# Queries and keys projected transposed, with even and odd columns apart, and rotated there

## The chip, the cores and the metric

The kernel runs on one core of one Trainium2 chip. Its time is the device time of one execution in microseconds (us), given as the median of several runs. The engines are TensorE (PE: matmuls and transposes), VectorE (DVE), ScalarE (ACT), GpSimd (POOL) and SyncE (SP), which issues most of the DMA transfers. The profile comes from one execution of its own.

## The reference

A transformer of four layers works on 1024 latent tokens and 256 context tokens of width 1024, in float32. Layers 0 and 3 are "banded": 16 query heads of 64 in four groups, each group with one key and value head, attention over a window of 128 tokens to either side and over the context, with a sink. Layer 1 is "latent": queries from a rank of 256, with 64 rotary dimensions in each of 8 heads. Layer 2 is an mLSTM. Queries and keys of latent tokens are rotated in pairs of neighbouring columns; context tokens are not rotated. The last layer needs no outputs for the context.

```python
def apply_rope(x, cos, sin):
    x1, x2 = x[..., 0::2], x[..., 1::2]
    cos, sin = cos[:, None, :], sin[:, None, :]
    return jnp.stack([x1 * cos - x2 * sin, x1 * sin + x2 * cos], axis=-1).reshape(x.shape)
...
    def block(n):
...
        logits = jnp.einsum('bqkgd,bjkd->bkgqj', q_b, k_b).astype(jnp.float32) * scale
        p = sink_softmax(jnp.where(mask, logits, NEG_INF), sink_l)
        return jnp.einsum('bkgqj,bjkd->bqkgd', p.astype(v_b.dtype), v_b)
...
    y_l = (o_l * jax.nn.silu(z_l)) @ w_out
```

## The kernel before

A float32 product is made of three matmuls on parts of type float32r: high by high, high by low and low by high (`split` makes the parts, one engine the high and another the low one). The normed input lies transposed in the on-chip memory for the whole layer, `hT` = (`hh`, `hl`), channels on partitions and 1280 tokens in a row. Weights come in as pieces of 512 KB, in one stream whose order `plan` fixes; `step` splits a piece into `wh` and `wl`, `need` takes pieces up to a given chunk, and a `pacer` does so bit by bit between other work. The columns of the modulation (`mod_piece`, tiles `raw` and `cs`) come in the same stream. Code is written in one order, and a scheduler then sets each engine's own order from it.

A banded layer (`layer_a`) has these stages. Keys and values: for each of ten token tiles of 128, 24 matmuls of 512 columns give keys and values token by token. `rope` rotates the keys (a VectorE product with the cosine, two with the sine and an add on GpSimd), `kv_back` splits them, and a tile later `kv_tr` transposes high and low parts (8 transposes, an ACT copy) and stores them to DRAM (`kd`). In layer 0 the norm of the input tiles (`first_norm`) feeds these tiles one by one, and the pacer takes up gate columns of the modulation and the first z weights between them. Then come eight z blocks (`z_block`), and then group 0's queries.

The attention runs over units (group, token tile): ten tiles in each of four groups in layer 0, eight in layer 3. Unit s does scores and weights (`stage_s`) while unit s - 1 transposes its weights and multiplies them by the values (`stage_pv`). Between the parts `fill` puts steps of the next group's query projection (`proj_q`): 24 matmuls of 256 columns for a token tile, three to a step. The projected tile is rotated by `rope` and stored row by row (`qd`). For each unit `load_q` brings its queries back two units ahead, and `stage_q` splits them (`q2`), transposes them for four heads, and copies them to `qT`, [128 = high and low parts of 64 dimensions, 4 heads x 128 tokens]. In the last group there is nothing to project; the output weights are split in its place.

In the latent layer (`layer_b`) `uq_front` and `uq_back` project, rotate, split and transpose the rotary queries of all heads for one token tile at a time, between the z blocks: eight transposes a tile.

## Time and profile before

| | us |
|---|---|
| median of 3 runs | 3097.39 |
| lowest and highest | 3097.36, 3098.17 |
| span of the profiled execution | 3100.0 |
| TensorE busy in it | 2904.0 |
| VectorE, ScalarE, GpSimd busy | 1751.2, 1315.9, 1271.3 |

The span runs from the first to the last instruction of the profiled execution; no other time is known of that execution, and its span is 2.6 us above the median of the runs. A busy engine need not be a full one: matmuls overlap, so the distance from one start to the next tells more than their durations. A stretch is a part of the span in which one stage runs, and an idle engine has a releaser, the work whose end it waited for.

### The profile page before, as it was taken

The numbers are of one execution on the slowest core, as the hardware profiler recorded it, in microseconds if no ns is written. First come the engines' busy times: TensorE is split into PE (matmuls) and PEld (weight loads), VectorE is DVE, ScalarE is ACT, GpSimd is POOL, SyncE is SP. The second block draws the span as 40 slices with busy tenths as digits, with TensorE's granted clock in tenths as the row PEclk, the third lists the DMA queues.
The fourth block names the chain that finished last, engine by engine and source line by source line (L and its number), as shares of the span: only waits on it lengthen the run. The fifth ranks groups of instructions, "written<-read, shape, count | busy, mean of one in ns | idle before, by whom it ended". The sixth has DMA issues, their size and how long they took to land. (4 is left out here: it accounts for less than half of the span.)

```text
span 3100.0 us, 51341 instructions
## 1 busy us (share of the span) xinstructions
PE 2904.0 (94%) x18340; PEld 2542.3 (82%) x18340; DVE 1751.2 (56%) x4001; ACT 1315.9 (42%) x2812; POOL 1271.3 (41%) x1584
## 2 busy tenths in 40 slices
PE   7999999999999999999898999998888999999998
PEld 4788888778888788888787899998776778988877
DVE  3413877875522466666456644244497742588862
ACT  2311776763322355555433323132364431367662
POOL 2413666655643010100454331246574532466652
PEclk9999999999999999999999999999898999999999
DMA  7563222434246211111443344688576545232313
GB/s 230 177 195 109 73 77 88 143 116 133 90 150 187 78 43 33 33 40 32 129 143 118 118 148 134 212 292 292 196 244 214 180 129 176 70 93 88 103 60 119
DMA packets 404386, 409.52 MB, mean 132 GB/s; under 512 B 29506, under 2 KB 351322, under 8 KB 403106
## 3 DMA queue, kind: packets, MB, share of 16 engines
q1 hardware_dynamic: 398816, 399.25, 40.3%
q10 hardware_dynamic: 4882, 6.33, 0.6%
q8 instruction: 145, 2.38, 0.3%
q0 software_dynamic: 432, 0.66, 0.1%
q14 instruction: 111, 0.91, 0.1%
HBM read 275.46 MB, written 131.34 MB: 131 GB/s over the span
## 5 line engine op out<-in xcount | busy, mean ns | idle before, releaser
L89 DVE TENSOR_TENSOR pl<-n,ph 128x512 fp32r<-128x512 f32 x488 | 330.4, 685 | 94.6 <-ACT ph L80 79.7
L80 ACT ACTIVATE ph<-n 128x512 fp32r<-128x512 f32 x488 | 285.1, 596 | 156.9 <-PE n L75 92.0
L72 PE MATMUL n<-ph,v 128*128 128x256 f32 (+1 forms) x992 | 292.3, 337 | 15.1 <-ACT ph L80 9.0
L75 PE MATMUL n<-ident,p 128*128 128x128 f32 x1952 | 289.5, 277 | 8.5 <-DVE o L846 4.8
L72 PE MATMUL n<-wh,hh 128*128 128x256 f32 x960 | 278.4, 290 | 16.3 <-DVE sg L1659 11.7
L812 POOL TENSOR_SCALAR p<-p,rl 128x640 f32<-128x640 f32 (+2 forms) x288 | 215.8, 762 | 167.1 <-DVE rl L810 114.1
L72 PE MATMUL n<-wl,hh 128*128 128x256 f32 x960 | 275.4, 287 | 0.0
L72 PE MATMUL n<-wh,hl 128*128 128x256 f32 x960 | 275.1, 287 | 0.0
L805 ACT ACTIVATE p<-p,nm 128x641 f32<-128x641 f32 (+2 forms) x288 | 220.7, 767 | 121.7 <-DVE nm L803 111.0
L75 PEld LDWEIGHTS n<-ident,p 128*128 128x128 f32 x1952 | 234.6, 142 | 43.7 <-issue 10.8
L72 PE MATMUL n<-pl,v 128*128 128x512 f32 (+1 forms) x656 | 241.6, 368 | 9.7 <-DVE pl L89 8.7
L801 DVE CUSTOM_DVE_ANT_0 p<-w,mask 128x640 f32<-128x640 f32 (+2 forms) x288 | 209.5, 744 | 60.3 <-PE w L72 51.6
L72 PE MATMUL n<-hh,wh 128*128 128x512 f32 (+1 forms) x656 | 242.1, 369 | 0.0
L89 POOL TENSOR_TENSOR wl<-raw,wh 128x1024 fp32r<-128x1024 f32 x54 | 135.9, 2521 | 253.6 <-DVE wh L82 180.5
L72 PE MATMUL n<-hl,wh 128*128 128x512 f32 (+1 forms) x656 | 238.4, 363 | 0.0
L72 PE MATMUL n<-hh,wl 128*128 128x512 f32 (+1 forms) x656 | 238.2, 363 | 0.0
L72 PE MATMUL w<-ks,qT 128*128 128x256 f32 (+1 forms) x1088 | 204.0, 316 | 17.9 <-DVE mx L801 13.5
L1232 POOL TENSOR_TENSOR o<-o,z 128x256 f32<-128x256 f32 x40 | 30.4, 760 | 447.5 <-ACT o L1231 204.2
L72 PEld LDWEIGHTS n<-wh,hh 128*128 128x128 f32 x960 | 187.8, 196 | 20.3 <-DVE sg L1659 12.7
L72 PEld LDWEIGHTS n<-ph,v 128*128 128x128 f32 x992 | 175.6, 190 | 29.6 <-ACT ph L80 17.6
L72 PEld LDWEIGHTS w<-ks,qT 128*128 128x128 f32 x1088 | 172.6, 192 | 29.5 <-DVE mx L801 18.4
L72 PEld LDWEIGHTS n<-wl,hh 128*128 128x128 f32 x960 | 187.8, 196 | 0.1
(333 smaller groups left out, 7598.3 us busy)
## 6 DMA issues: line engine op xcount, KB each, us to landing
raw<-in_l_w_ada_dram SPq DMA_DIRECT2D x96, 512.0 KB
raw<-in_l_w_in_dram SPq DMA_DIRECT2D x72, 512.0 KB
raw<-in_l_w_out_dram SPq DMA_DIRECT2D x32, 512.0 KB
vd<-v SPq DMA_DIRECT2D x60, 256.0 KB
xd<-xt SPq DMA_DIRECT2D x30, 512.0 KB
od<-o SPq DMA_DIRECT2D x112, 128.0 KB
go<-od SPq DMA_DIRECT2D x28, 512.0 KB
xt<-xd SPq DMA_DIRECT2D x28, 512.0 KB
```

What stands on the lines that cost most here:

```text
L72: self.nc.tensor.matmul(out, lhsT, rhs, start=start, stop=stop)
L75: self.nc.tensor.transpose(out, in_, self.ident)
L80: nc.scalar.activation(out=out, in_=in_, func=AF.Copy)
L89: e.tensor_tensor(out=lo, in0=src, in1=as32(hi), op=ALU.subtract)
L801: nc.vector.tensor_tensor_reduce(out=p[:, 0:n], in0=ps[:, s0:768], in1=mask[:, mo:mo + n], scale=1.0, scalar=-3.0e38, op0=ALU.add, op1=ALU ...
L805: nc.scalar.activation(out=p[:, 0:n + 1], in_=p[:, 0:n + 1], func=AF.Exp, scale=0.125, bias=nm[:, j:j + 1], accum_out=lsum[:, j:j + 1])
L812: nc.gpsimd.tensor_scalar(out=pr[y][:, 0:n], in0=pr[y][:, 0:n], scalar1=rl[:, y:y + 1], scalar2=0.5, op0=ALU.mult, op1=ALU.mult)
L1232: nc.gpsimd.tensor_tensor(out=o, in0=o, in1=z, op=ALU.mult)
```

## The change

The weights of keys, queries and rotary queries are put into another column order when they are split: first the even dimensions of all heads, then the odd ones (`Chunk.eo`, `take`). With these as the fixed operand and `hT` as the moving one, a matmul gives [128 = 4 heads x 32 even dimensions, up to 512 tokens]. The pieces of tokens are `PIECES` = ((0, 512), (512, 512), (1024, 256)). `eo_even` copies the even half out of PSUM; `eo_odd` multiplies the odd half by sine and cosine on VectorE (tables laid out transposed, `cosT` and `sinT`) and the even half on GpSimd, combines them, splits both results into high and low parts (`eo_h`, `eo_l`, one buffer each) and stores each part to DRAM. `load_q` and `load_group` put them together as [parts and halves, heads, tokens], so that `rope` on queries, `kv_back`, `kv_tr`, `stage_q`, `uq_front` and `uq_back` fall away. The values are still projected token by token, with 256 columns; the keys follow in pieces, in `keys`. In layer 0 the z weights get their place, and the pacer starts, only after the last tile. A step of `fill` is now one matmul.

```diff
-        qd = [self.pd.tile([T, 256], F32, name=f"qd{i}_{g}") for g in range(4)]
-        kd = self.pd.tile([4, 128, 2, T], F32, name=f"kd{i}")
+        qd = [self.pd.tile([4, 128, T], F32, name=f"qd{i}_{g}") for g in range(4)]
+        kd = self.pd.tile([4, 128, T], F32, name=f"kd{i}")
...
+    def take(self, ch, rv, k0, s, hi, lo):
+        k = slice(k0, k0 + s)
+        eo = ch.eo
+        if eo:
+            def paired(a):
+                a = a[:, :, 0:eo] if eo < ch.n else a
+                return a if eo == 256 else a.rearrange("p k (a c) -> p (k a) c", c=256)
+            o = [paired(w[:, k]).rearrange("p k (b j) -> p k b j", b=2) for w in (ch.wh, ch.wl)]
+            self.split(o[0], o[1], paired(rv).rearrange("p k (j b) -> p k b j", b=2), hi, lo)
+        if eo < ch.n:
+            self.split(ch.wh[:, k, eo:ch.n], ch.wl[:, k, eo:ch.n], rv[:, :, eo:ch.n], hi, lo)
...
+    def eo_even(self, pool, ps, t0, n):
+        e = pool.tile([128, 512], F32, name="eo_e", bufs=1)
+        self.nc.scalar.activation(out=e[:, 0:n], in_=ps[:, 0:n], func=AF.Copy)
+        return e
+
+    def eo_odd(self, pool, e, ps, t0, n, put):
+        nc = self.nc
+        e, ps = e[:, 0:n], ps[:, 0:n]
+        lat = t0 < NLAT
+        if lat:
+            c, sn = self.cosT[:, t0:t0 + n], self.sinT[:, t0:t0 + n]
+            x = [pool.tile([128, 512], F32, name=f"eo_t{x}", bufs=1)[:, 0:n] for x in range(3)]
+            nc.vector.tensor_tensor(out=x[0], in0=ps, in1=sn, op=ALU.mult)
+            nc.vector.tensor_tensor(out=x[1], in0=ps, in1=c, op=ALU.mult)
+            nc.gpsimd.tensor_tensor(out=x[2], in0=e, in1=sn, op=ALU.mult)
+            nc.gpsimd.tensor_tensor(out=e, in0=e, in1=c, op=ALU.mult)
+            nc.gpsimd.tensor_tensor(out=e, in0=e, in1=x[0], op=ALU.subtract)
+        for b in range(2):
+            hi, lo = [pool.tile([128, 512], F32R, name=f"eo_{x}", bufs=1)[:, 0:n] for x in "hl"]
+            if b and lat:
+                nc.vector.tensor_tensor(out=x[2], in0=x[2], in1=x[1], op=ALU.add)
+            self.split(hi, lo, e if b == 0 else x[2] if lat else ps, "act", "pool" if b == 0 or lat else "dve")
+            for p, y in ((b, hi), (b + 2, lo)):
+                nc.sync.dma_start(out=put(p)[:, t0:t0 + n], in_=as32(y))
...
-        pend = None
+        def keys(t0, n):
+            w = P["kv"]
+            e = None
+            for b in range(2):
+                ps = self.psn()
+                self.proj_T(ps[:, 0:n], hT, w.wh, w.wl, 128 * b, 128, t0, n)
+                if b == 0:
+                    e = self.eo_even(qp, ps, t0, n)
+                else:
+                    self.eo_odd(qp, e, ps, t0, n, lambda p: kd[p])
+
+        stretches = {1: [PIECES[2]], 5: [PIECES[0]], 9: [PIECES[1]]}
+        if i:
+            stretches = {1: [PIECES[2]], 9: [PIECES[0], PIECES[1]]}
...
+            if n == (1 if i else NT - 1):
...
                 pz = self.pool("pz", hs)
                 for x in range(8):
                     P["z", x].place(pz, 2)
-                go = self.pacer(NT - 2, P["z", 0])
-            elif n:
+                go = self.pacer(NT - 2 if i else 1, P["z", 0])
+            elif n > 1 and i:
                 go()
+            for x in stretches.get(n, ()):
+                keys(*x)
+        go()
...
-        fs, fp = ((3, 2, 2, 0), (0, 1, 0, 0, 0)) if need_ctx else ((2, 2, 2, 0), (0, 2, 0, 0, 0))
+            for t0, m in ((PIECES[2],) if need_ctx else ()) + PIECES[:2]:
+                e = None
+                ts = slice(t0, t0 + m)
+                for b in range(2):
+                    ps = self.psn()
+                    c = slice(128 * b, 128 * b + 128)
+                    for k in range(8):
+                        for x, (a_, b_) in enumerate(((w.wh, hh), (w.wh, hl), (w.wl, hh))):
+                            self.mm(ps[:, 0:m], a_[:, k, c], b_[:, k, ts], k == 0 and x == 0, k == 7 and x == 2)
+                            if k < 7 or x < 2:
+                                yield
+                    if b == 0:
+                        e = self.eo_even(qp, ps, t0, m)
+                    else:
+                        self.eo_odd(qp, e, ps, t0, m, lambda p: qd[g][p])
+                    yield
+
+        fs, fp = ((5, 4, 3, 0), (0, 2, 0, 0, 0)) if need_ctx else ((4, 3, 3, 0), (0, 2, 0, 0, 0))
...
         def load_q(u):
...
-            q = p2.tile([128, 4, 64], F32, name="qin", bufs=2)
-            nc.sync.dma_start(out=q, in_=qd[g][t * 128:(t + 1) * 128, :].rearrange("p (h d) -> p h d", d=64))
+            q = p2.tile([128, 4, 128], F32R, name="qT", bufs=2)
+            for p in range(4):
+                nc.sync.dma_start(out=as32(q[32 * p:32 * p + 32]),
+                                  in_=qd[g][p, :, t * 128:(t + 1) * 128].rearrange("(h i) t -> i h t", i=32))
```

In the attention of layer 0, TensorE's order has a run of query projections (`wqh` and `wql` the weights' parts) between the scores of a unit (`w<-ks,qT`) and the products with the values (`ph`, `pl` by `v`). Before, the run is 24 long at this place and of 256 columns, and the transposes of the next unit's queries come soon after:

```order
L72 MATMUL n<-ph,v_2187 128x512
L72 MATMUL n<-wqh,hh 128x256
L72 MATMUL n<-wql,hh 128x256
...
L72 MATMUL n<-wqh,hl 128x256
L72 MATMUL w<-ks,qT 128x384 x2
L72 MATMUL w<-ks,qT 128x256 x2
L72 MATMUL n<-pl,v_2187 128x512
L72 MATMUL n<-ph,v_2187 128x512
L75 MATMUL n<-ident,q_2935 128x128 x4
```

After, at the same place, the run is 19 long and of 512 columns:

```order
L73 MATMUL w<-ks,qT 128x384 x2
L73 MATMUL w<-ks,qT 128x256 x2
L73 MATMUL n<-pl,v_2142 128x512
L73 MATMUL n<-ph,v_2142 128x512
L73 MATMUL n<-hh,wqh 128x512
L73 MATMUL n<-hl,wqh 128x512
L73 MATMUL n<-hh,wql 128x512
...
L73 MATMUL n<-hh,wqh 128x512
L73 MATMUL n<-pl,v_2142 128x512
L73 MATMUL n<-ph,v_2142 128x512
L76 MATMUL n<-ident,p 128x128 x4
```

The transposes of queries are gone; the runs are wider, and there are fewer of them.

ScalarE's order in the same attention has the copy and the split of the queries among the exponentials (`p,lsum<-p,nm`) and the copies of the transposed weights (`ph<-n`). Before:

```order
L805 ACTIVATE p,lsum<-p,nm 128x641 x2
L765 ACTIVATE qT<-n 128x512
L80 ACTIVATE q_3084<-qin 128x4x64
L805 ACTIVATE p,lsum<-p,nm 128x641
L841 ACTIVATE up<-n 64x512
L80 ACTIVATE ph<-n 128x512 x2
```

After, `eo_h<-eo_e` is the high part of a piece's even half and `eo_h<-eo_t` that of its odd half:

```order
L81 ACTIVATE ph<-n 128x512 x3
L81 ACTIVATE eo_h<-eo_e 128x512
L81 ACTIVATE ph<-n 128x512
L81 ACTIVATE eo_h<-eo_t_4435 128x512
L81 ACTIVATE ph<-n 128x512
L852 ACTIVATE p,lsum<-p,nm 128x641 x2
```

The two high parts go into one buffer, with one weight copy between them.

At the end of layer 0's keys, TensorE's order after the change has the last keys (`wkvh`, `wkvl`), then modulation columns (`raw,cs`), then the first z block (`hh,wh`); before, the modulation columns stood between the tiles:

```order
L73 MATMUL n<-hh,wkvl 128x512
L73 MATMUL n<-raw,cs 32x256 x8
L73 MATMUL n<-sel,part 128x2 x2
L73 MATMUL n<-raw,cs 32x256 x4
...
L73 MATMUL n<-raw,cs 32x256 x4
L73 MATMUL n<-sel,part 128x2 x2
L76 MATMUL n<-ident,gc 16x128
L73 MATMUL n<-hh,wh 128x512
```

The modulation's last columns have moved behind the keys.

## Rows read from the trace of the kernel before

**Rows 1.** The profile's page: the span, the busy time of each engine with its share and instructions, and the chain that ended last by engine and line.
```profile
span 3100.0 us, 51341 instructions
PE 2904.0 (94%) x18340; PEld 2542.3 (82%) x18340; DVE 1751.2 (56%) x4001; ACT 1315.9 (42%) x2812; POOL 1271.3 (41%) x1584
...
PE n L72 18%; PE w L72 6%; PE n L75 3%; DVE acc L1328 1%; DMA e<-rmd 1%; DMA raw<-in_l_w_in_dram 1%; DVE cl L89 1%; POOL hl L89 1%; DMA kt<-ktd 1%; DVE big L374 1%; DMA gdd<-e 1%; DMA sgd<-sg 0%; DVE p L801 0%; DVE go L1782 0%; DMA dT<-gdd 0%
```

**Rows 2.** Busy time by stretch. Columns: start and end, length, busy us and instructions of PE, PEld (weight loads), DVE, ACT and POOL, then the granted TensorE clock, the DMA engines' mean busy share and GB/s. The stretches in turn: keys and values of layer 0, its group 0's queries, its attention for groups 0 to 2, most of the latent layer's z blocks, keys and values of layer 3, its attention for groups 0 to 2, and its last group.
```profile
49.10:137.30 88.20, 82.20 (x458) 66.36 (x458) 45.65 (x135) 32.05 (x60) 46.40 (x42) 0.94 0.58 171
...
259.20:288.60 29.40, 29.36 (x246) 29.12 (x244) 6.54 (x24) 1.57 (x5) 5.90 (x8) 1.00 0.18 60
288.60:610.00 321.40, 306.76 (x2148) 275.97 (x2149) 257.68 (x743) 220.95 (x499) 201.70 (x356) 0.97 0.28 88
...
845.00:1000.00 155.00, 153.29 (x940) 127.34 (x940) 43.80 (x121) 38.73 (x91) 64.27 (x73) 1.00 0.54 166
2525.40:2576.10 50.70, 50.70 (x250) 41.91 (x250) 10.67 (x35) 12.61 (x30) 10.67 (x14) 1.00 0.46 129
...
2682.00:2901.70 219.70, 213.84 (x1554) 198.71 (x1555) 180.91 (x512) 156.27 (x336) 140.88 (x238) 1.00 0.27 84
2901.70:2991.00 89.30, 75.91 (x452) 64.22 (x451) 74.42 (x180) 59.79 (x130) 64.23 (x92) 0.92 0.30 95
```

**Rows 3.** TensorE's own sequence in layer 3's attention: start, duration, engine, line, operation, output and inputs, shapes, count. The first row is the four transposes of a unit's queries.
```profile
2707.80 0.60 PE L75 MATMUL n<-ident,q 128*128 128x128 f32 x4
2708.15 0.48 PE L72 MATMUL n<-ph,v 128*128 128x512 f32 x1
```

**Rows 4.** The same view: the end of layer 0's z blocks with the start of its query projection, 256 columns each, and 512 columns in layer 3's z blocks.
```profile
259.04 0.28 PE L72 MATMUL n<-hh,wl 128*128 128x256 f32 x1
259.16 0.28 PE L72 MATMUL n<-wqh,hh 128*128 128x256 f32 x1
...
2599.80 0.39 PE L72 MATMUL n<-hh,wh 128*128 128x512 f32 x1
...
2600.93 0.39 PE L72 MATMUL n<-hh,wl 128*128 128x512 f32 x1
```

**Rows 5.** TensorE's waits at the start of the attention, in layer 0 (260 to 300 us) and in layer 3 (2580 to 2685): the line that waited, what ended the wait, total us, number, longest.
```profile
PE w L72 <- ACT qT L765: 3.4, 2, 2.7
PE n L75 <- POOL q L89: 1.3, 1, 1.3
...
PE n L75 <- POOL q L89: 0.8, 1, 0.8
PE w L72 <- ACT qT L765: 0.7, 1, 0.7
```

**Rows 6.** TensorE's sequence over one tile of layer 3's keys and values, from the transposes of one tile's keys (`k`) to those of the next.
```profile
2537.40 1.04 PE L75 MATMUL n<-ident,k 128*128 128x128 f32 x8
...
2538.51 0.40 PE L72 MATMUL n<-wkvl,hh 128*128 128x512 f32 x1
...
2543.64 0.39 PE L72 MATMUL n<-wkvh,hl 128*128 128x512 f32 x1
2543.88 1.03 PE L75 MATMUL n<-ident,k 128*128 128x128 f32 x8
```

**Rows 7.** A group of like instructions over the whole span: count, busy us, mean ns of one, idle time of the engine just before. These are the transposes of queries, 288 in the two banded layers and 80 in the latent one.
```profile
L75 PE MATMUL n<-ident,q 128*128 128x128 f32 x368 | 61.1, 278 | 3.6 <-POOL q L89 3.6
```

**Rows 8.** One tile's norm in layer 0, on three engines: the modulation, the high part and the low part.
```profile
85.27 2.65 DVE L374 TENSOR_SCALAR big<-n,mod 128x128 f32<-128x128 f32 x8
...
87.95 1.06 ACT L80 ACTIVATE hh<-big 128x1024 fp32r<-128x1024 f32 x1 [1.76 <-DVE big L374]
...
89.09 2.39 POOL L89 TENSOR_TENSOR hl<-big,hh 128x1024 fp32r<-128x1024 f32 x1 [1.59 <-ACT hh L80]
```

**Rows 9.** Pieces of the chain that ended last: start, us from issue to landing, and the transfer. A weight piece of 512 KB, a store of 256 KB, and a store of queries of 128 KB.
```profile
1732.41 4.39 DMA raw<-in_l_w_in_dram
...
1876.35 2.13 DMA vd<-v
...
2918.40 6.08 DMA qd<-q
```

**Rows 10.** Groups of like instructions, by shape: over the whole span, and the last two rows over 300 to 600 us.
```profile
L245 POOL TENSOR_TENSOR q<-rope,rope 128x512 f32<-128x512 f32 x8 | 10.3, 1289 | 41.4 <-DVE rope L243 41.4
...
L238 DVE TENSOR_TENSOR rope<-n,cos 128x512 f32<-128x512 f32 x8 | 5.5, 692 | 15.5 <-PE n L72 15.5
...
L238 DVE TENSOR_TENSOR rope<-n,cos 128x256 f32<-128x256 f32 x80 | 33.8, 423 | 86.8 <-PE n L72 81.1 <-PE n L75 5.2
...
L243 DVE TENSOR_TENSOR rope<-n,sin 128x128 f32<-128x128 f32 x160 | 38.8, 282 | 0.0
...
L80 ACT ACTIVATE ph<-n 128x512 fp32r<-128x512 f32 x127 | 73.4, 595 | 20.1 <-DVE pl L89 6.8 <-DVE rl L810 5.5 <-PE n L75 4.0
...
L89 POOL TENSOR_TENSOR q<-qin,q 128x256 fp32r<-128x256 f32 x31 | 23.8, 767 | 11.1 <-ACT q L80 5.0 <-PE n L75 3.0 <-PE n L72 2.3
```

**Rows 11.** SyncE's issues of a unit's output, in layer 0's last group: one a unit.
```profile
653.18 0.46 SPq L848 DMA_DIRECT2D od<-o  x1
...
662.98 0.52 SPq L848 DMA_DIRECT2D od<-o  x1
```

More of the change, by code (lines that the diff above doesn't have):

```diff
@@ L286, in setup, with tables @@
         self.xd = self.pd.tile([T, D], F32, name="xd")
+    def tables(self, pool):
+        self.cosT = pool.tile([128, NLAT], F32, name="cosT")
+        self.sinT = pool.tile([128, NLAT], F32, name="sinT")
+        self.nc.scalar.dma_start(out=self.cosT, in_=self.ins["k_cosT"])
+        self.nc.scalar.dma_start(out=self.sinT, in_=self.ins["k_sinT"])
     def load_cols(self, i, queue):
@@ L742, in load_group @@
             ks = p2.tile([128, 2, T], F32R, name="ks", bufs=2)
-            nc.sync.dma_start(out=as32(ks), in_=kd[g])
+            for x in range(2):
+                for p in range(4):
+                    nc.sync.dma_start(out=as32(ks[32 * p:32 * p + 32, x]), in_=kd[(p + 2 * x) % 4, 32 * g:32 * g + 32, :])
             v2 = p2.tile([128, NT, 128], F32R, name="v2", bufs=2)
@@ L754, in load_q @@
                               .rearrange("(a p) t -> p a t", p=128))
-            st[u] = {"q": q, "z": z}
-        def stage_q(u):
-            q = st[u]["q"]
-            q2 = p3.tile([128, 4, 128], F32R, name="q2", bufs=1)
-            self.split(q2[:, :, 0:64], q2[:, :, 64:128], q, "act", "pool")
-            pt = self.psn()
-            for h in range(4):
-                self.tr(pt[:, h * 128:(h + 1) * 128], as32(q2[:, h, :]))
-            qT = p3.tile([128, 4, 128], F32R, name="qT", bufs=2)
-            nc.scalar.activation(out=qT, in_=pt[:, :].rearrange("p (h t) -> p h t", h=4), func=AF.Copy)
-            st[u]["qT"] = qT
+            st[u] = {"qT": q, "z": z}
         def cols(t):
@@ L889, in layer_a @@
                     load_group(units[s][0] + 1)
-                if s + 2 < nu and s + 2 not in st and (s + 2) % nq >= 2:
-                    load_q(s + 2)
                 stage_s(s, fill)
@@ L1079, in proj_q @@
             qp = p2.tile([128, 512], F32R, name="qp", bufs=2)
-            nc.sync.dma_start(out=as32(qp[:, 0:n]), in_=qpd[h, :, s])
+            for x in range(4):
+                nc.sync.dma_start(out=as32(qp[32 * x:32 * x + 32, 0:n]), in_=qpd[x, 32 * h:32 * h + 32, s])
             for t in range(t0 // 128, (t0 + n) // 128):
@@ L1098, in layer_b @@
         done = set()
-        uq = deque(ORDER)
-        upend = pu = None
+        uq = deque((hb, t0, n) for (t0, n) in PIECES for hb in range(2))
+        pu = None
         slot = 0
```

133 lines of the change are left out of this document (51 added, 82 removed).

## The prediction

> **What bounds the kernel now.** I read the page first: TensorE is busy for 94% of the span, and the chain that ended last runs through its matmuls more than through anything else [rows 1]. A share over the whole span says little, so the table of stretches came next [rows 2]. It splits into two kinds. The keys and values of the last layer, the z blocks of the latent layer and the first projection of a group of queries are dense: TensorE is busy for 50.70 of 50.70 us, 153.29 of 155.00 and 29.36 of 29.40. The attention of groups 0 to 2 is nearly dense, with 306.76 of 321.40 us in layer 0 and 213.84 of 219.70 in layer 3, at a granted clock of 0.97 and 1.00; VectorE comes second there (257.68 and 180.91). What is taken off TensorE in these places should come off the time. The other kind is the last group of queries, which has no projection between its units: 75.91 of 89.30 us on TensorE, 74.42 on VectorE. Nobody is full there and I count nothing for it. The keys and values of layer 0 are a third case (82.20 of 88.20), since a chain over three engines feeds them. Last I read the waits at the two places where the scores of group 0 begin, and single rows for the durations.
>
> **What the change removes.** *Transposes of queries.* Each unit loses four on TensorE, the split of its queries and the copy back. In the stream the four take 0.35 us, from 2707.80 to the next matmul at 2708.15 [rows 3]. Layer 0 has 30 units in groups 0 to 2 and layer 3 has 24: 54 x 0.35 = 18.9 us. The 18 units of the two last groups are set at nothing, because TensorE waits there anyway; at full worth they would be 6.3 more.
>
> *Projection of queries.* The moving operand grows from 256 columns to 512, except for the 256 context tokens. A matmul of 256 columns follows the one before after 0.12 us, one of 512 after (2600.93 - 2599.80) / 5 = 0.226 [rows 4]. A group of layer 0 goes from 240 x 0.12 = 28.8 us to 96 x 0.226 + 48 x 0.12 = 27.5, one of layer 3 from 192 x 0.12 = 23.0 to 96 x 0.226 = 21.7. Eight groups at 1.3 give 10.4 us. The keys of layer 3 show 0.233 for 512 columns [rows 6], at which the term is 5; the queries have the weights on the side where the z blocks have them, so I take 0.226. A rule speaks against the change here: the Trainium skill, page "TensorE: Matmul & The Clock Gate", section "Back-to-back issue gap", puts an isolated gap at N / 2.4 + 2.5 ns, by which I estimate 109 ns for 256 columns and 216 for 512, and half the instructions would save 0.25 us a group, 2 us in all. The trace has 120 and 226 and doesn't agree at 256.
>
> *The start of the attention.* TensorE now waits 3.4 + 1.3 us in layer 0 and 0.8 + 0.7 in layer 3 for the first queries to be split, transposed and copied [rows 5]. After the change they come ready from memory. In layer 0 the context piece is projected first, 2 x 10.9 us before group 0's projection ends, so the 4.7 us go. In layer 3 the first piece has 10.9 us, and its rotation, split, store (2.13) and load add up to about as much; I leave that wait where it is.
>
> *Keys.* In layer 3 a tile takes 6.48 us (2537.40 to 2543.88), and 24 matmuls at (2543.64 - 2538.51) / 22 = 0.233 are 5.60 of it; eight transposes are the other 0.88 [rows 6]. The columns of the matmuls stay the same: 24 of 512 a tile become 24 of 256 for the values and 48 for each piece of keys. The first two tiles wait for weights, which leaves 8 x 0.88 = 7.0 us.
>
> *Rotary queries of the latent layer.* 80 of the 368 transposes [rows 7] lie in a dense stretch, at 0.35 / 4: 7.1 us.
>
> *Keys of layer 0.* TensorE loses ten times 0.88, 8.8 us. But a tile's norm runs VectorE 2.65, ScalarE 1.06 and GpSimd 2.39 us in a row [rows 8], and the modulation's eight gate pieces, which lay between the tiles, now stand behind them with the first z weights. A 512 KB piece takes some 4.4 us to land [rows 9], and three are there in advance; casting the z piece and its low part adds 3. I estimate a tail of 12 us behind the last key matmul. That matmul would end near 49.1 + 82.2 - 8.8 = 122 and z begin near 134, against 137.3: 3.3 us gained. The bounds are 8.8 gained (the tail hidden) and 8.7 lost (a tail twice as long).
>
> Sum of gains: 18.9 + 10.4 + 4.7 + 7.0 + 7.1 + 3.3 = 51.4 us.
>
> **What it adds.** *Work off TensorE.* A piece of 512 tokens asks GpSimd for three products and two low parts at 1.29 us each [rows 10], 6.4 us, and VectorE for three at 0.69, which is 0.52 a tile where the old rotation had 0.42 and two of 0.28 (0.98). ScalarE loses a copy and a split a unit and gets three copies of 0.6 a piece, 0.45 a tile. GpSimd drops a split and an add of 0.77 each a tile for 1.6, so it stays where it is, at 0.63 of the stretch. All this lies under TensorE and costs nothing while TensorE is the bound. If that cover went, GpSimd's 6.4 us would stand in front of one store, needed half a group later.
>
> *Single buffers.* This is the cost I do charge. The rotated halves leave through one buffer for the high and one for the low part. The second half's high part, on ScalarE, must wait until the first half's store has landed. In the new order one weight copy of 0.6 us lies between the two on ScalarE, and on GpSimd nothing. Behind the waiting instruction stand the copies of the weights, and TensorE waits for those. A store of 256 KB, the size of these, landed in 2.13 us, a store of 128 KB in 6.08 [rows 9]. From the nearest row: 2.13 + 0.35 to issue - 1.0 of work between = 1.5 us. About half of the 15 pieces projected inside the attention have so little between: 7 x 1.5 = 11 us. Bounds: nothing, if ScalarE has that much slack (it is busy for 220.95 of 321.40 us), and 7 x 5.5 = 38.
>
> *Evenness.* Now a unit has one run of about 18 projection matmuls, 2.2 us; then a run is 19 of 512 columns, 4.3 us, every 1.8 units. During a run the softmax gets no scores. A unit without projection takes 9.8 us in the last group (653.18 to 662.98) [rows 11]; less 0.5 for the rotation, 9.3. Say u is the part of a run that nothing covers. Now 9.8 + 2.2 u = 541.1 / 54 = 10.0, so u is 0.1; then 9.3 + 4.3 u / 1.8 = 9.55 at the same u. TensorE's own sum gives 10.0 - 0.35 - 10.4 / 54 = 9.46. I take no extra cost.
>
> *Queues.* SP issues five transfers a unit for two, and four stores a piece for four row stores; at 0.4 to 0.5 us each that is 2.5 us of a unit of 10. Queries are loaded two units ahead, so a load that stands behind a waiting store has some 9 us to spare.
>
> 51.4 - 11 = 40.4 us. The profiled execution has a span of 3100.0 us, 2.6 above the median of 3097.4; the differences are taken from its rows and set against the median: 3097.4 - 40.4 = 3057.0 us. A difference under 0.2%, 6.2 us, can't be told from no change.
>
> **Rivals.**
> *Stores block ScalarE and GpSimd for their longest landing.* For it: the stores and the loads of queries share one queue, and 6.08 us occurs. Against it: DMA engines are 28% busy in that stretch. Price 38 instead of 11: 3084 us. It decides nothing about the sign. The Trainium skill, page "DMA: Bandwidth & Descriptors", section "Anatomy of one DMA — SWDGE (gpsimd) path", gives some 2 us of fixed cost to each transfer, mostly the receipt of the write. The 2.13 us row agrees.
> *Long runs starve the softmax (the slower side).* If u rises to 0.5, a unit takes 9.3 + 1.2 = 10.5, and 54 units lose 27 us while the other stretches gain 17.4: 3107 us. It decides from u = 0.43 on, which is 0.3 us a unit lost. For it: VectorE would be at 0.85 of the time between runs, and only two score buffers hold work. Against it: nine weight buffers, and u is 0.1 now.
> *A long tail behind layer 0's keys.* Modulation and the first z weights in a row, nothing beside them: 8.7 lost for 3.3 gained, 3069 us. For it: one modulation chunk can't be multiplied before it has landed, and TensorE has no other work there.
> *Wide matmuls bring nothing.* If the 0.12 us comes from what stands around these matmuls and not from their width, those of 512 would follow after 0.24 and the term of 10.4 is 0: 3067.4 us. For it: 0.233 in the keys. Against it: 0.226 in the z blocks, a stretch as dense. The rule of the page above would leave 2 of the 10.4.
>
> **How the numbers follow.** The forecast has 0.50, blocking stores 0.18, starving 0.17, the tail 0.10, even spacing 0.05. Below, the forecast reaches to 3057 - 11 (no store wait) - 5.5 (tail hidden) - 6.3 (last groups) = 3034. Above, 3090 takes in the blocked stores and leaves out most of the starving case, so 3032 to 3090 holds about 0.8; the forecast's own range is 3034 to 3070. Faster by more than 0.2%: 0.50 + 0.10 + 0.05, and 0.16 of the blocked stores: 0.81. Same: 0.02 of these and 0.07 of the starving: 0.09. Slower: 0.10.
>
> **What the profile after would show.** Transposes of queries and of keys gone from both banded layers; projections of queries at 0.226 us apart; a unit at about 9.5 us; the copy of the second half's high part released by the landing of the first half's store, some 1.5 us late; the first z matmul of layer 0 near 134. The prediction is wrong if TensorE's idle time in the stretch of 321.40 us grows beyond its 14.6 us by more than the 11, or if z begins after 137.3.

## The result and the profile after

The changed kernel takes 3126.98 us (median of 4 runs, 3119.02 to 3134.14) against 3097.78 before: a ratio of 1.0093, interval 1.0078 to 1.0107. It is 29 us slower where 40 us less were forecast. The profiled execution has a span of 3132.4 us. TensorE is busy for less time than in [rows 1], and the span is longer:

```profile
span 3132.4 us, 49280 instructions
PE 2872.5 (92%) x17344; PEld 2469.5 (79%) x17344; DVE 1728.8 (55%) x3807; ACT 1255.4 (40%) x2665; POOL 1286.8 (41%) x1527
```

Where it went shows in the length of each stage, from its first matmul to the first of the next stage. In the two profiles (us):

| stage | before | after | moved | forecast |
|---|---|---|---|---|
| up to layer 0's first key matmul | 49.1 | 53.2 | +4.1 | 0 |
| layer 0 keys, to the first z matmul | 88.1 | 104.0 | +15.9 | -3.3 |
| layer 0 z | 121.9 | 123.0 | +1.1 | 0 |
| layer 0 group 0's queries | 30.1 | 27.6 | -2.5 | |
| layer 0 attention, to the first output matmul | 385.4 | 387.7 | +2.4 | -14 with the row above |
| layer 0 from there to the latent layer's first matmul | 127.0 | 128.9 | +1.8 | |
| latent layer z | 164.8 | 166.4 | +1.6 | -7.1 |
| layer 3 keys | 71.6 | 75.9 | +4.3 | -7.0 |
| layer 3 group 0's queries | 24.4 | 22.7 | -1.7 | |
| layer 3 attention, to the first output matmul | 307.1 | 312.5 | +5.4 | |
| layer 3 from there to the last matmul | 107.7 | 107.8 | +0.1 | -9 with the two rows above |

The first row overstates its loss: in the other runs of the changed kernel the first key matmul began at 50.3 to 51.5 us, in those of the kernel before at 49.1 to 50.0.

The busy times by stretch, in the columns of [rows 2]: layer 0's keys, what follows them up to z, layer 0's attention (most of groups 0 to 2), the latent layer's z, the start of layer 3's keys, its attention.

```profile
53.20:137.90 84.70, 73.72 (x468) 64.83 (x472) 36.30 (x95) 24.06 (x40) 39.57 (x32) 0.96 0.33 100
137.90:157.20 19.30, 7.84 (x65) 4.07 (x65) 8.30 (x14) 1.26 (x2) 6.91 (x5) 0.67 0.94 277
...
307.80:627.00 319.20, 292.39 (x1705) 243.42 (x1703) 245.70 (x679) 200.73 (x446) 201.95 (x326) 0.98 0.38 115
...
886.60:1053.00 166.40, 157.20 (x950) 127.23 (x949) 44.06 (x104) 31.68 (x70) 58.94 (x49) 0.97 0.56 179
2517.50:2540.00 22.50, 10.50 (x54) 9.40 (x54) 16.90 (x27) 5.63 (x11) 15.78 (x13) 0.71 0.57 172
...
2703.10:2935.00 231.90, 217.69 (x1215) 181.21 (x1216) 183.93 (x470) 147.70 (x310) 148.73 (x221) 0.99 0.35 105
```

The stretches of the attentions do not end at the same work as those of [rows 2]. From the first scores to the first output matmul layer 0's attention has, before and then after:

```profile
289.25:674.60 385.35, 362.97 (x2522) 321.32 (x2523) 315.00 (x885) 267.63 (x595) 246.73 (x421) 0.97 0.32 101
...
307.82:695.55 387.73, 349.32 (x2079) 288.28 (x2078) 305.08 (x837) 245.34 (x540) 245.41 (x393) 0.97 0.41 126
```

It lost 13.7 us of TensorE's busy time, near the 14.4 counted, and did not get shorter: TensorE's idle time grew from 22.4 us to 38.4. TensorE's waits in the stretches of groups 0 to 2, before and then after (line, what ended the wait, total us, number, longest):

```profile
PE n L72 <- ACT ph L80: 1.7, 6, 0.7
...
PE n L72 <- DVE pl L89: 1.6, 2, 1.4
...
PE n L73 <- DVE pl L90: 13.1, 15, 2.1
PE n L73 <- ACT ph L81: 5.2, 8, 2.2
PE w L73 <- DVE mx L848: 3.7, 7, 1.6
PE n L76 <- DVE eo_t L276: 2.3, 3, 1.7
```

A unit in the middle of a group, by the issues of its output, went from 10.2 us (342.90 to 353.10 before) to 11.1. Others got shorter: over the first 38 outputs of layer 0 the mean distance went from 10.01 us to 10.15.

```profile
352.68 0.41 SPq L895 DMA_DIRECT2D od<-o  x1
363.80 0.41 SPq L895 DMA_DIRECT2D od<-o  x1
```

### The profile page after: what moved, and what is told of

It is laid out like the page before. It is cut to its first block, busy times and chain, and to the rows that moved or that the text cites. A ratio compares the mean times of both kernels' runs of the same rounds, so it can differ in the third digit from the quotient of the medians.

```text
span 3132.4 us, 49280 instructions
## 1 busy us (share of the span) xinstructions
PE 2872.5 (92%) x17344; PEld 2469.5 (79%) x17344; DVE 1728.8 (55%) x3807; ACT 1255.4 (40%) x2665; POOL 1286.8 (41%) x1527
## 5 line engine op out<-in xcount | busy, mean ns | idle before, releaser
L73 PE MATMUL n<-ph,v 128*128 128x256 f32 (+1 forms) x992 | 293.2, 338 | 20.6 <-ACT ph L81 14.4
L76 PE MATMUL n<-ident,p 128*128 128x128 f32 x1952 | 296.1, 276 | 12.6 <-DVE eo_t L276 3.9
L73 PE MATMUL n<-wh,hh 128*128 128x256 f32 x960 | 276.6, 288 | 19.4 <-DVE sg L1697 13.6
```

The lines of the kernel that those rows point to most:

```text
L73: self.nc.tensor.matmul(out, lhsT, rhs, start=start, stop=stop)
L76: self.nc.tensor.transpose(out, in_, self.ident)
```

## The experiments

Each starts from the changed kernel unless it says otherwise. Two things tell how finely they can be read. The part from the latent layer's first output matmul to layer 3's first key matmul, which no edit touches, took between 971 and 994 us in these runs, so stages are compared and not totals of single runs. Two edits leave the attentions' code alone (e1, x4): layer 0's took 382.1 and 386.6 us there against 387.7, layer 3's 330.2 and 331.0 against 330.9. Less than 6 us in the one and 1 us in the other therefore says nothing. In this table layer 3's attention runs to the first output matmul that goes to a buffer of scores (`w`). Before the change that matmul stands 23.6 us behind the first output matmul of all, after it 18.3, since `fill`, whose pace the change altered, hands out both. So this column compares runs of one kernel only: between before and after it hides the 5.4 us of the table above.

| run | ratio | layer 0 keys | z | attention | latent z | layer 3 keys | attention |
|---|---|---|---|---|---|---|---|
| before | 1 | 88.1 | 121.9 | 385.4 | 164.8 | 71.6 | 330.8 |
| after | 1.0093 | 104.0 | 123.0 | 387.7 | 166.4 | 75.9 | 330.9 |
| e1 | 1.0033 | 74.2 | 134.4 | 382.1 | 170.1 | 76.2 | 330.2 |
| e2 | 1.0056 | 104.7 | 124.1 | 380.0 | 160.4 | 75.8 | 334.8 |
| e3 | 1.0115 | 105.9 | 123.1 | 385.0 | 166.8 | 75.2 | 333.2 |
| e4 | 1.0020 | 103.9 | 123.2 | 367.7 | 169.4 | 76.0 | 319.6 |
| e5 | 1.0084 | 103.8 | 122.9 | 384.5 | 166.6 | 75.0 | 330.0 |
| e6 | 1.0039 | 104.3 | 122.9 | 374.8 | 167.0 | 75.7 | 318.8 |
| e7 | 1.0136 | 103.6 | 123.8 | 386.2 | 167.8 | 75.2 | 332.5 |
| e8 | 1.0087 | 103.3 | 123.7 | 384.5 | 169.6 | 76.3 | 330.3 |
| e9 | 1.0089 | 106.9 | 122.6 | 377.6 | 167.6 | 76.2 | 326.8 |
| e10 | 1.0089 | 106.1 | 123.0 | 382.4 | 166.4 | 76.0 | 331.8 |
| e11 | 1.0111 | 105.5 | 123.3 | 387.1 | 164.3 | 75.6 | 332.4 |
| b1 | 1.0024 | 76.2 | 134.4 | 377.4 | 160.6 | 76.1 | 331.6 |
| b2 | 1.0011 | 75.4 | 134.4 | 378.2 | 157.5 | 76.3 | 330.9 |
| x1 | 0.9960 | 104.0 | 122.7 | 367.0 | 167.3 | 75.3 | 317.0 |
| x4 | 1.0103 | 105.4 | 123.3 | 386.6 | 167.2 | 75.9 | 331.0 |
| x2, of before | 0.9924 | 88.4 | 121.9 | 364.4 | 165.6 | 71.6 | 326.2 |
| x3, of before | 0.9984 | 88.1 | 121.9 | 378.5 | 166.3 | 71.6 | 331.1 |
| x5, of before | 1.0127 | 88.8 | 121.9 | 400.9 | 167.0 | 71.6 | 352.3 |

**Layer 0's keys: the gate columns between the tiles (e1).**

```diff
-                mods(8, 12, 0)
+                P["gate"] = mods(8, 12, 0)[-1]
...
+                if i == 0:
+                    go = self.pacer(NT - 2, P["gate"])
...
-            elif n > 1 and i:
+            elif n > 1:
                 go()
```

> Layer 0's gate columns of the modulation are taken up between the key tiles again, as before the change; everything else stays as changed. Theory A (the tail behind the last key matmul, 19.3 us in which the DMA engines are 0.94 busy, is the transfer of these 4 MB and nothing else): z of layer 0 starts some 14 us earlier, near 143 instead of 157, and the whole gains 12 to 15 us, to about 3113. Rival B (the key tiles are bound by the norm's chain over VectorE, ScalarE and GpSimd, and work put between them lengthens them): less than 6 us gained.

Ratio 1.0033 (1.0020 to 1.0046). Keys and z together fall from 227.0 to 208.6 us, below the 210.0 before. (z begins at 124.5 there, ahead of the last piece of keys, whose matmuls are counted under z; that is why z takes 134.4.) TensorE's sequence after the change shows what stood there: it waits for the modulation's weights and then for the columns made of them, and z begins at 157.22.

```profile
148.12 1.08 PE L73 MATMUL n<-raw,cs 128*32 128x256 f32 x8 [6.43 <-DMA raw<-in_l_w_ada_dram]
...
157.20 0.37 PE L76 MATMUL n<-ident,gc 128*16 128x128 f32 x1 [2.89 <-DVE gc L388]
157.22 0.77 PE L73 MATMUL n<-hh,wh 128*128 128x512 f32 x1
```

The transfers are busy for 0.94 of those 19.3 us and for 0.33 of the 84.7 before; in e1 for 0.52 of the keys' stretch:

```profile
50.30:124.50 74.20, 62.44 (x461) 54.29 (x462) 41.45 (x106) 23.09 (x38) 40.67 (x32) 0.95 0.52 157
```

Of the two theories A holds, but not its "nothing else". Five of the eight modulation pieces were issued by 124.4 us, three of them before the keys. The other three were issued only from 139.0 on, behind two loads of values for the attention, 640 KB each, as SyncE's issues show:

```profile
137.93 1.05 SPq L801 DMA_DIRECT2D v<-vd  x2
139.03 5.50 SPq L148 DMA_DIRECT2D raw<-in_l_w_ada_dram  x3
```

How much of the tail these loads cost, no run shows.

**The chain behind a piece, nothing left out (e2, e3, e5, e8, e11).** e2 gives the odd half's parts other buffers, e3 makes the high parts where the half was made, e5 takes pieces of 256 tokens, e8 writes the chain's operations one by one between the next piece's matmuls (its diff is too long to show), e11 multiplies the even half on VectorE.

```diff
+            if not (b and lat):
+                hi, lo = [pool.tile([128, 512], F32R, name=f"eo_{x}", bufs=1)[:, 0:n] for x in "hl"]
             if b and lat:
+                hi, lo = x[0].bitcast(F32R), x[1].bitcast(F32R)
```

```diff
-            self.split(hi, lo, ..., "act", "pool" if b == 0 or lat else "dve")
+            self.split(hi, lo, ..., ("dve" if b else "pool") if lat else "act", "pool" if b == 0 or lat else "dve")
```

```diff
-            for t0, m in ((PIECES[2],) if need_ctx else ()) + PIECES[:2]:
+            for t0, m in ((PIECES[2],) if need_ctx else ()) + ((0, 256), (256, 256), (512, 256), (768, 256)):
```

```diff
+            self.nc.vector.tensor_tensor(out=self.x2[:, 0:n], in0=ps[:, 0:n], in1=self.sinT[:, t0:t0 + n], op=ALU.mult)
+            self.nc.vector.tensor_tensor(out=e[:, 0:n], in0=ps[:, 0:n], in1=self.cosT[:, t0:t0 + n], op=ALU.mult)
...
-            nc.gpsimd.tensor_tensor(out=x[2], in0=e, in1=sn, op=ALU.mult)
-            nc.gpsimd.tensor_tensor(out=e, in0=e, in1=c, op=ALU.mult)
```

> The odd half's high and low parts go into two buffers that are free by then, so that they need not wait for the even half's store. Theory R1 of the prediction (single buffers block ScalarE and GpSimd): the waits for the stores of high and low parts, 6.1 and 0.3 us on ScalarE and 5.1 on GpSimd in the two attentions, go, and the whole gains 10 us or more. Rival (these waits lie under TensorE's work, and what costs is the rest of the chain or the long runs): 3 us or less.

> The high parts of rotated halves are made by the engine that made the half (GpSimd for the even one, VectorE for the odd one) and no longer by ScalarE; ScalarE keeps the copy out of PSUM. Theory C (ScalarE works in order and stands behind a rotation that GpSimd finishes late, 20.7 us in the latent layer's z stretch and some in the attentions): the latent layer's z stretch falls from 166.4 to about 159, the two attentions by 5 to 10 us together, the whole to about 3112. Rival (GpSimd, with 0.62 us more a piece, or the long runs are what holds the attention): the z stretch falls, the attentions do not move by more than 3 us.

> Queries of the banded layers are projected in pieces of 256 latent tokens and not 512: runs of 24 x 0.12 = 2.9 us, operations of the chain of 0.77 us in place of 1.29, twice as many stores of 128 KB, and the 0.16 us a tile that the wide matmuls gained are lost, 10.4 us. Theory C (what counts is how long each burst is): the two attentions fall by more than 10 us together in spite of that. Theory E (the amount of work and the number of stores count): they grow by 5 to 15 us.

> The operations behind a projected piece of queries are written one by one between the matmuls of the next piece and no longer all at once; nothing is left out. Theory C1 (the burst on GpSimd, and behind it ScalarE, is what holds the softmax): the two attentions fall by 15 to 30 us together, the whole to about 3105. Rival (the scheduler moves each operation to where it is ready, so that the order of writing decides little): within 6 us of 718.6 us for the two.

> Both products of the even half go to VectorE, straight from PSUM, and ScalarE's copy of that half falls away; nothing is left out. A piece then costs VectorE 5 x 0.69 and GpSimd 3 x 1.29 us, 0.86 and 0.97 a tile, where the kernel before had 0.98 and 1.54. Theory G: the two attentions fall by 10 to 20 us together, the latent layer's z stretch from 166.4 to near 160, the whole to about 3105. Theory V: the attentions grow by 5 us or more.

e2 moves the latent layer's z to 160.4 us, where the runs without that edit have 164.3 to 170.1: the single buffers cost some 6 us there. In the attentions it gives 7.7 less and 3.9 more. Its ratio is 1.0056 (1.0036 to 1.0075), some 11 us less than the changed kernel, as R1 asked; but R1 put the waits into the attentions, and there it isn't borne out, all the less as e7 below, with no stores at all, leaves them as they were. The other four leave both attentions within 4 us of the changed kernel's, and their totals between 1.0084 and 1.0115. So neither the store, nor ScalarE's part, nor the bursts' place in the code, nor the share between GpSimd and VectorE sets the loss alone. Of the size of the bursts e5 says less: it also gave up the width of the matmuls, 10 us of TensorE's work by its own count, and neither of its theories came true. In e11 theory G falls, and theory V with it (387.1 and 332.4); theory C of e3, for ScalarE, falls too.

**Parts of the chain left out (e4, e6, e7, e9, e10).**

```diff
-                    if b == 0:
+                    if b == 0 or g:
                         e = self.eo_even(qp, ps, t0, m)
...
-                                  in_=qd[g][p, :, t * 128:(t + 1) * 128]
+                                  in_=qd[0][p, :, t * 128:(t + 1) * 128]
```

That is e4. For `g > 0`, e6 sets `lat` false, by which the odd half's low part also goes from GpSimd to VectorE, e7 skips the stores and reads `qd[0]`, e9 skips the three GpSimd operations ahead of the splits, e10 the two VectorE products and the sum.

> Left out: rotation, splits and stores of the queries of groups 1 to 3 in layers 0 and 3; their projections are copied out of PSUM and dropped, and the attention reads group 0's queries. TensorE's work stays the same. Theory C (the chain behind the projection holds up the softmax's engines): the two attentions fall from 387.7 and 330.9 us to about 373 and 320, TensorE's idle time in them to what it was before the change. Theory D (long runs of 512-column projections starve the softmax, whatever follows them): they stay within 4 us of 387.7 and 330.9.

> Left out: the rotation of the queries of groups 1 to 3 in layers 0 and 3 (two VectorE products and a sum, three GpSimd products a piece); splits and stores stay, the odd half's low part goes to VectorE. Theory C1 (GpSimd's bursts of up to five operations of 1.29 us hold up the normalising of the weights): the two attentions lose about as much as without any chain, 20 and 11 us, to near 370 and 322. Theory C2 (the stores and the loads that depend on them are what costs): they stay within 4 us of 387.7 and 330.9.

> Left out: the stores of the queries of groups 1 to 3 in layers 0 and 3, so the attention reads group 0's; rotation and splits stay. Theory C1 (GpSimd's bursts): the two attentions stay within 6 us of 387.7 and 330.9, where the second buffers gave 7.7 less and 3.9 more. Theory C2 (stores on SP, their landing, loads behind them): they fall to near 370 and 322.

> Left out: GpSimd's part of the rotation of the queries of groups 1 to 3 in layers 0 and 3 (two products and a difference, 3.9 us a piece); VectorE's two products and sum, the splits and the stores stay. Theory G (GpSimd is the late one): the two attentions fall to within 5 us of what they took without any rotation, 374.8 and 318.8 us. Theory V (VectorE's products from PSUM, 0.69 us each, cut into the softmax): they stay within 5 us of 387.7 and 330.9.

> Left out: VectorE's part of that rotation (two products and a sum, 2.07 us a piece); GpSimd's three operations, its two low parts and the stores stay. Theory G: the two attentions stay within 5 us of 387.7 and 330.9. Theory V: they fall to near 374.8 and 318.8.

With the chain gone, both attentions fall, by 20.0 and 11.3 us. From first scores to first output matmul in layer 0, the changed kernel and then e4:

```profile
307.82 0.51 PE L73 MATMUL w<-ks,qT 128*128 128x256 f32 x3
695.55 0.62 PE L73 MATMUL w<-wo0h,gh 128*128 128x512 f32 x2
```

```profile
305.65 0.51 PE L73 MATMUL w<-ks,qT 128*128 128x256 f32 x3
673.34 0.62 PE L73 MATMUL w<-wo0h,gh 128*128 128x512 f32 x2
```

So TensorE's order with its long runs, 21 matmuls at most in both, is not what holds the attention: theory D, and with it the starving rival, falls. The rotation is most of it (e6: 12.9 and 12.1), the stores are nothing (e7, whose high total comes from the part that no edit touches, 994 us there). GpSimd's part alone gives 10.1 and 4.1, VectorE's 5.3 and -0.9, the last two within what can't be told. So theory G comes near in layer 0 (377.6 for 374.8 without any rotation) and not in layer 3 (326.8 for 318.8).

**How much TensorE's work is worth (x1, x2, x3, x5).** x1 and x2 leave out one of the three matmuls of each query projection in groups 1 to 3 (x1 the one with the weights' low part, x2 the one with the input's), x3 the transposes, x5 the rotation; the last three in the kernel before.

```diff
-                            self.mm(ps[:, 0:m], a_[:, k, c], b_[:, k, ts], k == 0 and x == 0, k == 7 and x == 2)
+                            if g == 0 or x < 2:
+                                self.mm(ps[:, 0:m], a_[:, k, c], b_[:, k, ts], k == 0 and x == 0,
+                                        k == 7 and x == (1 if g else 2))
```

```diff
-            pt = self.psn()
-            for h in range(4):
-                self.tr(pt[:, h * 128:(h + 1) * 128], as32(q2[:, h, :]))
...
-            nc.scalar.activation(out=qT, in_=pt[:, :].rearrange("p (h t) -> p h t", h=4), func=AF.Copy)
+            nc.scalar.activation(out=qT, in_=as32(q2), func=AF.Copy)
```

```diff
-                self.rope(q32, ps[:, 0:256], t, 4, qp)
+                self.rope(q32, ps[:, 0:256], t if g == 0 else NTL, 4, qp)
```

> The changed kernel with one of the three matmuls of each query projection left out for groups 1 to 3 of layers 0 and 3 (the low part of the weights), its place in the order kept empty. TensorE's work falls by 48 x 0.23 + 24 x 0.12 a group and by 32 x 0.23 a group of layer 3, hence 29 and 22 us. Theory P (the attention still follows TensorE): the two attentions fall by 20 us or more each, from 387.7 and 330.9. Theory Q (after the change the softmax's engines and their order of work set the length of a unit, not TensorE): less than 8 us each.

> The kernel before with the same matmul of each query projection left out for groups 1 to 3 of layers 0 and 3: 80 x 0.12 us a group of layer 0 and 64 x 0.12 of layer 3 less on TensorE, 29 and 23 us. Theory P (TensorE was the bound, as the prediction read it): the two attentions fall by 20 us or more each, from 385.4 and 330.8. Theory Q' (it was no more the bound than the other engines): less than 8 us each.

> The kernel before without the four transposes of queries in each unit of layers 0 and 3: their input is copied to where their output would be, so the split and the copy stay. TensorE loses 0.35 us a unit. The prediction's first term: 10.5 us less in layer 0's attention and 8.4 in layer 3's. Theory Q': less than 4 us each.

> The kernel before with the rotation of the queries of groups 1 to 3 in layers 0 and 3 left out: a copy on ScalarE, 0.41 us a tile, stands for VectorE's 0.98 and GpSimd's 0.77. In the changed kernel the same omission took 12.9 and 12.1 us off the two attentions. Theory F (rotation costs the new form more than the old one: in few large operations it cuts into the softmax, in many small ones it fits): here it takes less than 6 us off each. Theory Q (rotation costs the softmax its time in either form, so saved matmuls were never the whole of it): 10 us or more off each.

Before the change, 28.8 us less on TensorE made layer 0's attention 21.0 us shorter (0.73), and 23.0 us less made layer 3's 4.6 shorter (0.20). The transposes, 10.5 and 8.4 us, were worth 6.9, which is little above what can be told, and -0.3. TensorE was the bound in layer 0 for the most part, and in layer 3 it was not, though it is busy there for 213.84 of 219.70 us [rows 2]. After the change 28 and 22 us are worth 20.7 and 13.9 (x1 leaves out 32 wide and 16 narrow matmuls a group of layer 0, not the 48 and 24 of its expectation). x5 answers its question with neither theory: a copy of some 0.4 us a tile on ScalarE in place of the old rotation makes the attentions 15.5 and 21.5 us longer, although VectorE and GpSimd do less. What the old rotation cost is thereby left open.

**Layer 3's keys (x4).**

```diff
+            wide = i == 3 and n < 2
+            vc = slice(0, 512) if wide else slice(256, 512)
...
-                self.mm(ps[:, 0:256], hh[:, k, tk], w.wh[:, k, 256:512], k == 0, False)
...
+                self.mm(vp, hh[:, k, tk], w.wh[:, k, vc], k == 0, False)
...
```

> The first two key tiles of layer 3 multiply all 512 columns again, and the keys' half is not used: 48 x 0.11 = 5.4 us more on TensorE. Theory A (these tiles lie beside the split of the weights and the norm of the last tiles of the layer before, which set their time, and TensorE waits there now): the stretch of keys and values stays at 75.9 us within 1.5. Rival (the finer split of the weights is what delays): it grows by 4 to 6 us.

75.9 us with 5.4 us more work: TensorE's work does not set the time of these tiles, as theory A says. The first two tiles lie beside the weights' split and the norm of the layer before's last tiles, and TensorE waits for these after the change:

```profile
2521.05 0.58 PE L73 MATMUL n<-wkvl,hh 128*128 128x256 f32 x1 [3.06 <-DVE wkvl L90]
...
2532.30 0.39 PE L73 MATMUL n<-wkvl,hh 128*128 128x256 f32 x1 [2.32 <-POOL wkvl L90]
2538.93 1.97 PE L76 MATMUL n<-ident,big 128*128 128x128 f32 x8 [5.18 <-DVE big L403]
```

Before, the keys of these tiles were multiplied in that time; after, their matmuls come behind it.

The longest of these waits, 5.18 us for `big`, has a cause that the expectation does not name. `big` needs the norm's `rs` of GpSimd, and after the change the low part of the first z weights (`wl`) stands in front of it. Before, it came behind. GpSimd before, and then after:

```profile
2506.44 0.55 POOL L97 TENSOR_TENSOR rs<-ms,mhalf 128x1 f32<-128x1 f32 x1
...
2517.13 5.13 POOL L89 TENSOR_TENSOR wl<-raw,wh 128x1024 fp32r<-128x1024 f32 x2 [4.68 <-DVE wh L82]
...
2532.93 4.65 POOL L90 TENSOR_TENSOR wl<-raw,wh 128x1024 fp32r<-128x1024 f32 x2
2537.54 0.54 POOL L98 TENSOR_TENSOR rs<-ms,mhalf 128x1 f32<-128x1 f32 x1
```

All runs with the changed keys have this order, x4 among them. What follows the first two tiles starts 18.8 us into the stage before and 23.1 after, and takes 52.8 us in both. No run moves the z weights back.

**What is understood, put right (b1, b2).** b1 has e1, e2 and e11; b2 has e5 too, and splits the values' weights ahead of the keys':

```diff
+        if eo < ch.n:
+            self.split(ch.wh[:, k, eo:ch.n], ch.wl[:, k, eo:ch.n], rv[:, :, eo:ch.n], hi, lo)
         if eo:
...
-        if eo < ch.n:
-            self.split(ch.wh[:, k, eo:ch.n], ch.wl[:, k, eo:ch.n], rv[:, :, eo:ch.n], hi, lo)
```

> Gate columns between the key tiles, buffers of their own for the odd half's parts, and the even products on VectorE, together. Theory G: 18.6 + 4 + 20 us less than the changed kernel, about 3085, faster than the kernel before by 0.4%. Theory V: about 3105, slower than before.

> The three edits of b1 (gate columns between the key tiles, buffers of their own for the odd half, even products on VectorE), pieces of 256 latent queries, and the weights of the values split ahead of those of the keys. b1 took 1.0024 of the time before. If short runs and early values each give the 4 us that the traces show, it comes to about 0.9997 of it, 3096; if short runs cost their 10 us of matmuls, 1.005.

b1 comes to 1.0024 (1.0013 to 1.0034), near the 3105 us of theory V, though e11 had not borne that theory out; b2 to 1.0011 (1.0001 to 1.0021). Both are close to the kernel before, and not ahead of it. Early values bring nothing in layer 3's keys (76.3). No complete version beat the kernel before.

## Why the prediction was wrong, point by point

**"What is taken off TensorE in these places should come off the time."** This is the step that failed in the attentions. The work did go: 13.7 us of busy time in layer 0's attention. By the slopes of x2, if they hold for it, the 14.4 and 12.3 us of transposes and projections were worth 10.5 and 2.5 us of time, and not 27. A busy share of 0.95 or 0.97 was read as a bound, when matmuls that wait overlap in the record: x2 took out 23.0 us of layer 3's matmuls, at their distance of 0.12, and the busy time of that attention fell from 310.4 to 299.3. The attentions grew by 2.4 and 5.4 us, so by the same slopes the new form added some 13 and 8.

**"All this lies under TensorE and costs nothing."** It failed too. Without the chain the attentions take 20.0 and 11.3 us less, so it costs time, and enough of it to outweigh the saved matmuls. The old form had a chain of its own, whose price x5 leaves open, so how much of this is new isn't shown. One price in it was wrong, the sum on VectorE of two operands from SBUF (0.69 us taken, 1.56 and 1.78 in the mean of the two stretches, below). That is 0.9 to 1.1 us a piece, 13 in the two stretches, and no more than a part of the loss. How the rest comes about, over three engines that each work in order, the runs don't settle: e9 and e10 split it, e3, e8 and e11 shift it, and none of them finds one engine.

**Single buffers.** The mechanism is there, and in the wrong place: e2 and e7 show little of the 11 us in the attentions, while the latent layer, where I charged nothing, has 6 of them. There ScalarE stands with the next piece's copy and the next z block's tanh behind it. Of the chain it waits for the rotated even half most of all, and for the store:

```profile
ACT eo_h L81 <- POOL eo_e L279: 20.7, 4, 7.0
...
ACT eo_h L81 <- DMA qpd<-eo_h: 4.8, 3, 2.0
```

With that undone z takes 160.4, 160.6 and 157.5 us in e2, b1 and b2: 4 to 7 of the forecast 7.1 us are there. The Trainium skill, page "TensorE: Matmul & The Clock Gate", section "Architectural detail: the array is 16× 32×32, not 1× 128×128", has ScalarE's and VectorE's queues as strictly in order. The trace agrees as far as it goes: ScalarE does nothing in these waits, the longest of 7.0 us. The 2 us for each transfer that the prediction takes from the Trainium skill, page "DMA: Bandwidth & Descriptors", section "Anatomy of one DMA — SWDGE (gpsimd) path", are given there for transfers that GpSimd issues; the stores here are SyncE's.

**The start of the attention.** The wait that was to go in layer 0 went: none for `qT` is left there, where 3.4 us were before.

**Keys of layer 0.** The largest miss, +20 for -3.3 with the start. Three terms were wrong. The start came 4.1 us late in this profile, which I had not looked at, and some 1 us in the other runs: the tables and the finer split of the weights lie there, though no run takes them apart. The end of the keys came at 137.7 and not at 122, because I took TensorE's busy time for the length of the stage. The busy time itself came as counted (73.7 us for 73.4), but 11.0 us of waiting go with it, where 6.0 were before. After the change TensorE waits for the norm with nothing to fill the gaps:

```profile
PE n L73 <- POOL hl L90: 9.2, 8, 1.9
...
PE n L73 <- ACT hh L81: 3.5, 4, 2.2
```

The norm waits for TensorE in its turn: a tile's transposes at 105.04 come right behind a run of key matmuls that began at 94.08. And the tail is 19.4 us and not 12, with the last three modulation pieces issued behind the loads of values (e1). The rival of a long tail had 0.10. It came true at more than its price, and with 18.6 us by e1 it is the largest single part of the 29; without it the kernel is still slower, at 1.0033.

**Keys of layer 3.** 7.0 us counted, 4.3 lost. The arithmetic of the columns was right, but the first two tiles were hidden work, and half of it, 5.4 us, was moved to where nothing hides it; that eats most of the 7.0. The 4.3 us themselves are the later end of the first two tiles. In the traces that is the wait for the norm behind the z weights on GpSimd; the prediction had no term for it, and no run tests it.

**Width.** From start to start the projections of layer 0's groups 1 to 3 took 90.9 us before and 88.1 after, 0.9 us a group for the 1.3 counted; 512 columns follow each other after 0.231 us there. The term was right but for three tenths, and the rival of even spacing falls. By the rule of the Trainium skill, page "TensorE: Matmul & The Clock Gate", section "Back-to-back issue gap", the prediction's estimate was 0.25 a group; the trace doesn't agree.

**The starving rival** gave the right sign by another mechanism; e4 keeps the long runs and is fast.

Both signs of being wrong that the prediction named appeared: z began at 157.2, and TensorE's idle time in layer 0's attention grew by more than 11 us.

## What to carry to other kernels

A busy share near 1 doesn't say what a saved microsecond is worth: leave out a known amount of work on that engine alone and read the slope, before the savings are summed up. When a stage's code moves, look at what the weight stream was doing in that stage, since a load that was spread over ten tiles and now stands behind them has nothing to hide under. Look, too, at what the scheduler now puts in front of a short operation that another engine waits for. Work on TensorE under another chain's wait can be free, as 5.4 us were in x4; to take it from there saves nothing.

## What was not expected of the hardware

The sum of two SBUF tiles on VectorE took more than twice as long in the mean as a product with one operand in PSUM. Groups of like instructions in layer 0's attention after the change:

```profile
L283 DVE TENSOR_TENSOR eo_t<-eo_t,eo_t 128x512 f32<-128x512 f32 x7 | 10.9, 1558 | 0.2
...
L275 DVE TENSOR_TENSOR eo_t<-n,sinT 128x512 f32<-128x512 f32 x7 | 4.8, 685 | 0.0
```

In layer 3's it took 1780 ns in the mean. That mean hides two values. Of its six sums there three took 2.88 to 2.89 us and three 0.68. The long ones run beside GpSimd's split of query weights (`wql`), and the first ends 0.55 us after it; in the short ones GpSimd does nothing. GpSimd, VectorE and TensorE at such sums:

```profile
2703.04 5.12 POOL L90 TENSOR_TENSOR wql<-raw,wqh 128x1024 fp32r<-128x1024 f32 x2 [1.14 <-DVE wqh L83]
...
2705.83 2.88 DVE L283 TENSOR_TENSOR eo_t<-eo_t,eo_t 128x512 f32<-128x512 f32 x1
...
2733.61 0.68 DVE L283 TENSOR_TENSOR eo_t<-eo_t,eo_t 128x512 f32<-128x512 f32 x1
...
2777.98 2.89 DVE L283 TENSOR_TENSOR eo_t<-eo_t,eo_t 128x512 f32<-128x512 f32 x1
...
2781.53 1.35 PE L73 MATMUL w<-ks,qT 128*128 128x256 f32 x8 [1.95 <-DVE mx L848]
```

The Trainium skill, page "SBUF — State Buffer", section "Who interferes with whom", says that a VectorE instruction with two SBUF inputs contends with a GpSimd instruction that reads SBUF. The trace agrees, and e9 too: with GpSimd's three operations gone, three of layer 0's sums took 0.69 us that had taken 1.27 to 1.34 beside them. TensorE waited 1.95 us for scores whose maximum stood behind the sum at 2777.98. How much of the chain's 20.0 and 11.3 us comes this way, no run shows.

TensorE's clock fell to 0.50 of full speed, the lower of its levels (1.2 GHz), in the first wait of 3.06 us at the start of layer 3's keys, with matmuls running on at that level (start and end, length, then as in [rows 2]). The second row is the first 22.5 us of the stage before the change, at 1.00:

```profile
2522.00:2526.00 4.00, 3.70 (x18) 3.41 (x17) 4.00 (x10) 1.06 (x1) 1.76 (x2) 0.50 0.49 151
...
2492.50:2515.00 22.50, 17.74 (x82) 13.45 (x81) 15.78 (x29) 8.65 (x16) 11.29 (x10) 1.00 0.54 162
```
